# First conditioning of a two-layer mixer kernel: four two-column products at four column tiles in one step

## The chip, the cores and the metric

The kernel runs on one core of one Trainium2 chip. The metric is the device time of the program in microseconds (us). Before the change it is 2925.82 us, the median of three runs (2924.45, 2925.82, 2926.82). A profile of one more execution gives the time of every instruction; the engines in it are PE (matrix products), PEld (loading of the stationary operand of a product), DVE and ACT (elementwise work and copies out of PSUM), POOL (here mostly a queue that issues DMA transfers) and SP (the other such queue).

## The reference, cut to what matters

The program computes two layers of a diffusion backbone over 1024 latent tokens and 256 context tokens, 1024 channels each. The part that changes is the conditioning at the very start. Six vectors of 1024 numbers per layer come out of one product of a conditioning vector with a 1024 x 6144 matrix, and the first two of them (shift and scale) are wanted before the first normalized input exists:

```
def ada_mod(cond, w, b):
    m = (jax.nn.silu(cond) @ w + b)[..., None, :]
    return jnp.split(m, 6, axis=-1)

sh1, sc1, g1, sh2, sc2, g2 = ada_mod(c, ada_w[i], ada_b[i])
u_lat = modulate(rms_norm(h_lat, norm1_g[i]), sh1, sc1)
csh1, csc1, cg1, csh2, csc2, cg2 = ada_mod(c_ctx, ada_w[i], ada_b[i])
u_ctx = modulate(rms_norm(h_ctx, norm1_g[i]), csh1, csc1)
```

There are two conditioning vectors, `c` and `c_ctx`, so the stationary operand of each product has two columns only. In the same stage of the program stands `hyena_filters`: a small network of two sine layers, a product with `w3`, a decaying window, and then the spectrum of the filter, which the kernel makes as products with cosine and sine matrices.

## The kernel before, in words

One class, `Builder`, writes the whole program. A scheduling layer then decides, from the order in which the code is written, from the buffers and from its own costs, in which order each engine receives its instructions; the order inside an engine's queue is fixed from then on, and an engine waits at the head of its queue.

The first 80 us hold four pieces of work, which `run` interleaves by taking steps of generators:

- `ada_first` (L408 to L436). The matrix for scale (m = 1) and shift (m = 0) lies in DRAM as 16 blocks of 128 x 1024 (512 KB each), `in_ada_k`, for two values of m and eight blocks kb of the contraction. Each block goes into a tile `mat`, which takes the two buffers of tag `wh` and the two of tag `wl` in turn, so that four blocks are in the core at a time. The POOL queue issues the loads (`ldr`, L274). For each block there are two products (L416 to L421) with two columns of `cond`, each over 512 of the 1024 outputs, j = 0 and 1, accumulated over kb into two PSUM tiles `ps`. The operands are 32-bit floats. After the eight blocks of m = 1, ACT copies the two rows out of PSUM (L426), eight small products with the identity turn them into columns (L429), and DVE adds the bias. Then the same for m = 0. A generator step is one block; `run` takes eight steps first and then one between any two steps of the filter.
- `filter_mlp` (L561) and `filter_raw` (L607): the sine layers, then 32 products with `w3`, each multiplied by DVE with a window tile `in_win_l` (L641) on its way out of PSUM. `in_win_l` has eight tiles of 256 KB, which the SP queue loads.
- `norms` (in `run`): ten tiles `in_x_row` of 512 KB on the SP queue, squared and summed on ACT (L2144), and three products that spread the result over partitions (`ps` from `t` and `tk`, copied out at L2157).
- `filter_spectrum` (L679): per step, a block of a cosine or sine matrix, `in_ff_l` (256 KB, 16-bit), is loaded by SP into a tile `cs` and cast by ACT to a tile `mat` (L335). These `mat` tiles use the same four buffers as the blocks of `in_ada_k`, and `cs` has two buffers. The operands `s` are made by DVE (L708) and split by ACT (L287) and DVE (L289). Per step come fourteen products, accumulated over b = 0 to 3.

PSUM has six buffers `ps` and two buffers `pq`. Behind this stage stand the second half of the filter spectrum together with the normalized input (L550 to L553), then the input projection from about 202 us on.

Of the kernel before, what the change touches and what calls it, by code (L numbers as in the profile page):

```python
# [10 lines left out]
F32 = mybir.dt.float32  # L11
# [10 lines left out]
KB = D // P  # L22
# [179 lines left out]
class Builder:  # L202
# [205 lines left out]
    def ada_first(self):  # L408

        nc, a = self.nc, self.a  # L410
        cond = self.C(16)
        self.ld(cond, a["cond"])
        nc.scalar.activation(cond, cond, AF.Silu)
        yield
        for m in (1, 0):
            ps = [self.PP(), self.PP()]  # L416
            for kb in range(KB):
                w = self.mat(1024, F32)
                self.ldr(w, a["ada_k"][m, kb])
                for j in (0, 1):  # L420
                    self.mm(ps[j][0:2, :], cond[:, 2 * kb:2 * kb + 2], w[:, j * 512:(j + 1) * 512], kb == 0, kb == KB - 1)  # L421
                yield
            col = self.PS()
            for j in (0, 1):
                row = self.G()
                nc.scalar.copy(row[0:2, :], ps[j][0:2, :])  # L426
                for k in range(4):
                    nb = 4 * j + k
                    self.mm(col[:, 2 * nb:2 * nb + 2], row[0:2, k * P:(k + 1) * P], self.ident[0:2, 0:2], True, True)  # L429
            sl = slice(m * 8, m * 8 + 8)  # L430
            for c in (0, 1):
                t = self.ada[(0, c)]
                nc.vector.tensor_tensor(t[:, sl], col[:, 0:16].rearrange("p (n c) -> p c n", c=2)[:, c],
                                        self.adab[:, sl], ADD)
                if m == 1:
                    nc.vector.scalar_tensor_tensor(t[:, sl], t[:, sl], 1.0, self.gs[:, 0:8], op0=ADD, op1=MUL)  # L436
# [1680 lines left out]
    def run(self):  # L2117
        nc, a = self.nc, self.a
# [10 lines left out]
        def drain(g):  # L2129
            for _ in g:  # L2130
                pass
# [59 lines left out]
        next(fr)  # L2191
        next(ng)
        drain(mlp)
        for _ in range(8):
            next(ada1)
        with self.tc.issue_after(self.clamp), self.tc.issue_after(self.sin):
            next(fr)
# [309 lines left out]
```

## Time and profile before

| | us |
|---|---|
| median of three runs | 2925.82 |
| the profiled execution | 2922.39 |
| its span, first to last instruction | 2920.6 |
| DVE busy | 2094.0 |
| ACT busy | 1647.9 |
| POOL busy | 641.4 |
| mean DMA rate over the span | 211 GB/s |
| mean granted clock of the matrix engine | 0.98 |

The page gives busy time per engine, and then groups of instructions by line, by operation and by tile name, buffer numbers left out. A name at the start of a row is the program's: `mat` is a block of weights, `c` a small constant tile (here `cond`), `s`, `t`, `tk` are working tiles. A 32-bit product is done in two passes, so that one product of the program is two MATMUL rows and two LDWEIGHTS rows of the trace. The granted clock is the share of full speed that the chip gave the matrix engine in a stretch.

### The profile page before, as it was taken

How to read it: one execution, taken by the hardware profiler on the slowest of the kernel's cores; microseconds unless marked ns; L12 is line 12 of the kernel's file. 1: busy time of each engine (PE TensorE's matmuls, PEld its weight loads, DVE VectorE, ACT ScalarE, POOL GpSimd, SP SyncE). 2: the span in 40 equal slices, each digit the busy share in tenths (PEclk: the TensorE clock that was granted, in tenths of full speed). 3: DMA queues.
4: the chain of work that ended last, by engine and by line, in shares of the span. 5: the costliest groups of instructions: out<-in, count | busy, mean ns of one | idle time of the engine just before them, and what ended most of it. 6: DMA issues, size and time to landing. Idle time of an engine off the chain costs nothing. (4 is left out here: it accounts for less than half of the span.)

```text
span 2920.6 us, 46051 instructions
## 1 busy us (share of the span) xinstructions
PE 2777.4 (95%) x16163; PEld 1710.9 (59%) x16163; DVE 2094.0 (72%) x3833; ACT 1647.9 (56%) x2899; POOL 641.4 (22%) x1057
## 2 busy tenths in 40 slices
PE   7889999999989999999999999999999999999998
PEld 3766557878879644444555844677665444444554
DVE  5678867585367798877886777777676778775765
ACT  4675325453675666654555555677664477654553
POOL 1012013354220111123120012454443022112000
PEclk9999999999999999999999999999999999999999
DMA  7574435358685555565995798777775666425753
GB/s 263 182 272 161 156 123 158 110 160 287 257 348 192 207 209 195 201 218 218 332 332 174 267 343 296 171 188 180 184 198 187 238 226 232 152 94 183 237 193 115
DMA packets 325156, 615.98 MB, mean 211 GB/s; under 512 B 90934, under 2 KB 130552, under 8 KB 324922
## 3 DMA queue, kind: packets, MB, share of 16 engines
q1 hardware_dynamic: 252378, 384.38, 40.4%
q0 software_dynamic: 70240, 224.45, 21.5%
q10 hardware_dynamic: 2304, 4.20, 0.4%
q8 instruction: 127, 2.08, 0.3%
q14 instruction: 107, 0.88, 0.1%
HBM read 455.33 MB, written 135.53 MB: 202 GB/s over the span
## 5 line engine op out<-in xcount | busy, mean ns | idle before, releaser
L1444 PE MATMUL ps<-s,s 128*128 128x512 f16 x2592 | 583.2, 382 | 15.8 <-ACT tk L1449 7.2
L1444 PEld LDWEIGHTS <-s 128*128 128x128 f16 x2640 | 258.9, 98 | 334.6 <-issue 30.3
L283 PE MATMUL ps<-s,wh 128*128 128x256 f32 (+3 forms) x1752 | 395.7, 329 | 13.1 <-ACT wh L287 7.3
L1213 ACT ACTIVATE s<-s,c 128x512 f16<-128x512 f32 (+1 forms) x324 | 233.3, 753 | 137.9 <-DMA s<-d 75.8
L1661 PE MATMUL ps<-s 128*128 128x512 f16 (+2 forms) x1308 | 305.0, 379 | 2.0 <-DVE s L1214 2.0
L1214 DVE SCALAR_TENSOR_TENSOR s<-s,c,s 128x512 f16<-128x512 f32 (+1 forms) x324 | 247.4, 794 | 78.3 <-ACT s L1213 77.7
L283 PE MATMUL pq<-s,wh 128*128 128x512 f16 (+1 forms) x1000 | 282.0, 356 | 12.2 <-DMA wh<-d 4.7
L283 PEld LDWEIGHTS <-wh 128*128 128x128 f16 x1664 | 160.3, 99 | 172.7 <-issue 24.7
L283 PE MATMUL ps<-s,wl 128*128 128x256 f32 (+3 forms) x876 | 260.2, 330 | 1.0 <-DVE wl L289 0.9
L274 POOL DMA_DIRECT2D d<-s x201 | 109.0, 543 | 660.5 <-DVE s L1505 193.1
L1661 PEld LDWEIGHTS <-s 128*128 128x128 f16 x1536 | 148.7, 98 | 179.5 <-issue 7.1
L283 PE MATMUL ps<-s,s 128*128 128x65 f16 (+5 forms) x2666 | 220.5, 235 | 20.2 <-DMA s<-s 8.2
L335 ACT CAST mat<-cs 128x1024 fp32r<-128x1024 f16 (+2 forms) x120 | 111.6, 935 | 139.0 <-PE ps L283 56.7
L283 PEld LDWEIGHTS ps<-s,wh 128*128 128x128 f32 x1088 | 178.0, 193 | 20.0 <-ACT wh L287 8.3
L283 PE MATMUL ps<-s,mat 128*128 128x512 f32 x696 | 182.8, 410 | 4.0 <-ACT s L287 3.0
L1444 PE MATMUL ps<-s,wh 128*128 128x512 f16 x616 | 185.0, 379 | 1.5 <-DVE g L1458 1.5
L283 PE MATMUL pq<-s,wl 128*128 128x512 f16 (+1 forms) x500 | 174.9, 355 | 1.6 <-DMA wl<-d 1.1
L283 PEld LDWEIGHTS <-s 128*128 128x128 f16 x2400 | 114.8, 98 | 79.5 <-DMA s<-s 9.1
L283 PEld LDWEIGHTS ps<-s,mat 128*128 128x128 f32 x696 | 135.4, 197 | 38.5 <-ACT s L287 4.4
L1246 ACT ACTIVATE t<-s 128x1024 bf16<-128x1024 f32 (+1 forms) x164 | 141.7, 866 | 14.4 <-DVE c L465 12.1
L1213 ACT ACTIVATE s<-t,c 128x512 f16<-128x512 f32 x172 | 115.1, 712 | 26.1 <-DVE c L1312 15.0
L283 PEld LDWEIGHTS ps<-s,s 128*128 128x128 f32 (+1 forms) x746 | 112.2, 190 | 27.6 <-DVE st L2039 4.2
(431 smaller groups left out, 5449.2 us busy)
## 6 DMA issues: line engine op xcount, KB each, us to landing
s<-d SPq DMA_DIRECT2D x294, 256.0 KB, 4.3
d<-s POOLq DMA_DIRECT2D x157, 256.0 KB, 3.2
s<-in_down SPq DMA_DIRECT2D x154, 256.0 KB, 5.4
s<-in_ada_w POOLq DMA_DIRECT2D x48, 512.0 KB, 5.0
g<-in_bias POOLq DMA_DIRECT2D x128, 192.0 KB, 3.3
s<-in_gate SPq DMA_DIRECT2D x46, 512.0 KB, 3.8
s<-in_up SPq DMA_DIRECT2D x46, 512.0 KB, 3.8
d<-g POOLq DMA_DIRECT2D x87, 256.0 KB, 3.0
```

The lines of the kernel that those rows point to most:

```text
L274: self.last_ldr = self.nc.gpsimd.dma_start(out, in_).ins
L283: self.nc.tensor.matmul(o, l, r, start=st, stop=sp)
L335: self.nc.scalar.copy(m, st)
L1213: nc.scalar.activation(hi, src, AF.Copy, scale=scale)
L1214: nc.vector.scalar_tensor_tensor(lo, src, scale, hi, op0=MUL, op1=SUB)
L1246: self.nc.scalar.activation(junk[:, :t.shape[1]], t, AF.Abs, scale=2.0 ** -15, accum_out=st[:, k:k + 1])
L1444: nc.tensor.matmul(ps, x[:, sl], y, start=first and j == 0 and x is wh and y is xh, stop=j == 3 and x is wl, skip_group_check=True)
L1661: m = nc.tensor.matmul(acc[j][:, c0:c1], x[:, sl], y[:, xs], start=first and k == 0, stop=last and k == 2, skip_group_check=True)
```

## The change

`ada_first` now takes both matrices and both halves in one step: for each kb it loads two blocks and issues four products, which write to four different places of one PSUM tile, partitions 0, 32, 64 and 96. The place of the output selects the columns of the array, so the four products of a step use four different strips of 32 columns. The rows are copied out only when all eight steps are done, first for m = 1 and then for m = 0. `run` takes four steps first, instead of eight, so the number of blocks ahead of the filter is the same.

```
-        for m in (1, 0):
-            ps = [self.PP(), self.PP()]
-            for kb in range(KB):
-                w = self.mat(1024, F32)
-                self.ldr(w, a["ada_k"][m, kb])
+        ps = self.PP()
+        for kb in range(KB):
+            ws = [self.mat(1024, F32) for _ in range(2)]
+            for m in (0, 1):
+                self.ldr(ws[m], a["ada_k"][m, kb])
+            for m in (0, 1):
                 for j in (0, 1):
-                    self.mm(ps[j][0:2, :], cond[:, 2 * kb:2 * kb + 2], w[:, j * 512:(j + 1) * 512], kb == 0, kb == KB - 1)
-                yield
+                    q = 32 * (2 * m + j)
+                    nc.tensor.matmul(ps[q:q + 2, :], cond[:, 2 * kb:2 * kb + 2], ws[m][:, j * 512:(j + 1) * 512],
+                                     start=kb == 0, stop=kb == KB - 1, skip_group_check=True)
+            yield
+        for m in (1, 0):
             col = self.PS()
             for j in (0, 1):
+                q = 32 * (2 * m + j)
                 row = self.G()
-                nc.scalar.copy(row[0:2, :], ps[j][0:2, :])
+                nc.scalar.copy(row[0:2, :], ps[q:q + 2, :])
...
-        for _ in range(8):
+        for _ in range(4):
             next(ada1)
```

Lines of the changed kernel behind this place have numbers five higher (L2157 becomes L2162, L426 becomes L431).

The scheduling layer moves other instructions too. On PE, at the end of these products, before: `ps_275` is the accumulator of m = 0, `mat_391` to `mat_409` are its last three blocks, `ps_366` and `ps_375` spread the norms, `ps_381` and `ps_401` are filter products, and `pq_464` is the first product of the spectrum.

```order
L283 MATMUL ps_366<-tk_361,c_91 128x512
L283 MATMUL ps_375<-tk_370,c_91 128x512
L283 MATMUL ps_275<-mat_391,c_115 2x512
L283 MATMUL ps_276<-mat_391,c_115 2x512
L283 MATMUL ps_381<-s_72_226,s_52_172 128x512
L283 MATMUL ps_381<-s_73_227,s_52_172 128x512
L283 MATMUL ps_275<-mat_405,c_115 2x512
L283 MATMUL ps_276<-mat_405,c_115 2x512
L283 MATMUL ps_401<-s_75_232,s_53_173 128x512
L283 MATMUL ps_401<-s_76_233,s_53_173 128x512
L283 MATMUL ps_275<-mat_409,c_115 2x512
L283 MATMUL ps_276<-mat_409,c_115 2x512
```

And the same place on PE after: `ps_190` is the one accumulator, `ps_346` and `ps_363` receive the columns, then come the three products for the norms and the last four filter products; the spectrum begins behind the last of these rows.

```order
L423 MATMUL ps_190<-mat_329,c_115 2x512 x2
L283 MATMUL ps_346<-c_86,g_347 128x2 x4
L283 MATMUL ps_346<-c_86,g_353 128x2 x4
L283 MATMUL ps_363<-c_86,g_364 128x2 x4
L283 MATMUL ps_363<-c_86,g_370 128x2 x4
L283 MATMUL ps_381<-t_378,c_91 128x256
L283 MATMUL ps_390<-tk_385,c_91 128x512
L283 MATMUL ps_399<-tk_394,c_91 128x512
L283 MATMUL ps_417<-s_71_225,s_53_173 128x512
L283 MATMUL ps_417<-s_72_226,s_53_173 128x512
L283 MATMUL ps_421<-s_74_231,s_53_173 128x512
L283 MATMUL ps_421<-s_75_232,s_53_173 128x512
```

So work that stood among the products of the conditioning now stands behind them: all four groups of columns, the norms and the last filter products.

On the SP queue, at the last two window tiles, before:

```order
L268 DMA s_109_340<-in_win_l 128x512
L268 DMA cs_497<-in_ff_l 128x1024
L268 DMA s_122_379<-in_win_l 128x512
L268 DMA s_128_395<-in_win_l 128x512
L268 DMA cs_521<-in_ff_l 128x1024
L268 DMA cs_549<-in_ff_l 128x1024
```

And at that place of the SP queue after, with the same loads under other numbers:

```order
L268 DMA s_107_336<-in_win_l 128x512
L268 DMA cs_494<-in_ff_l 128x1024
L268 DMA cs_518<-in_ff_l 128x1024
L268 DMA cs_546<-in_ff_l 128x1024
L268 DMA cs_623<-in_ff_l 128x1024
L268 DMA s_125_403<-in_win_l 128x512
L268 DMA s_130_415<-in_win_l 128x512
```

The last two window tiles moved from behind one `in_ff_l` load to behind four. Each of these loads needs a free `cs` buffer, that is, an earlier cast on ACT.

On ACT, between the casts of the first and the fourth matrix block of the spectrum (`mat_456`, `mat_520`), after:

```order
L335 CAST mat_456<-cs_454 128x1024
L335 CAST mat_472<-cs_470 128x1024
L431 COPY g_347<-ps_190 2x512
L431 COPY g_353<-ps_190 2x512
L431 COPY g_364<-ps_190 2x512
L431 COPY g_370<-ps_190 2x512
L335 CAST mat_496<-cs_494 128x1024
L335 CAST mat_520<-cs_518 128x1024
L2162 COPY s_118_383<-ps_381 128x256
L2162 COPY s_121_392<-ps_390 128x512
L2162 COPY s_124_401<-ps_399 128x512
```

Before, two of the four row copies stood earlier, ahead of the norms, and the other two behind the third cast. Now all four stand ahead of the third and the fourth cast, which the SP loads above wait for.

More of the change, by code (lines that the diff above doesn't have):

```diff
@@ L414, in ada_first @@
         yield
-        for m in (1, 0):
-            ps = [self.PP(), self.PP()]
-            for kb in range(KB):
-                w = self.mat(1024, F32)
-                self.ldr(w, a["ada_k"][m, kb])
-                for j in (0, 1):
-                    self.mm(ps[j][0:2, :], cond[:, 2 * kb:2 * kb + 2], w[:, j * 512:(j + 1) * 512], kb == 0, kb == KB - 1)
-                yield
+        ps = self.PP()
[4 more added lines that the diff above has]
+            for m in (0, 1):
+                for j in (0, 1):
+                    q = 32 * (2 * m + j)
+                    nc.tensor.matmul(ps[q:q + 2, :], cond[:, 2 * kb:2 * kb + 2], ws[m][:, j * 512:(j + 1) * 512],
+                                     start=kb == 0, stop=kb == KB - 1, skip_group_check=True)
+            yield
+        for m in (1, 0):
             col = self.PS()
             for j in (0, 1):
+                q = 32 * (2 * m + j)
                 row = self.G()
-                nc.scalar.copy(row[0:2, :], ps[j][0:2, :])
+                nc.scalar.copy(row[0:2, :], ps[q:q + 2, :])
                 for k in range(4):
```

## The prediction

> **What bounds the kernel now.** I read the page first, for the span and the busiest engine.
>
> ```profile
> span 2920.6 us, 46051 instructions
> PE 2777.4 (95%) x16163; PEld 1710.9 (59%) x16163; DVE 2094.0 (72%) x3833; ACT 1647.9 (56%) x2899; POOL 641.4 (22%) x1057
> ```
>
> PE is busy for 95% of the span, so PE time taken out of a stretch in which PE has no gap can reach the end. Then the windows: the first stage in tens of us (the columns after the window are its length and busy time of PE, PEld, DVE, ACT, POOL, then granted clock, DMA share, GB/s), and the stretches behind it.
>
> ```profile
> 20.00:30.00 10.00, 8.89 (x24) 2.61 (x23) 8.18 (x14) 5.92 (x12) 2.69 (x5) 1.00 1.05 409
> 30.00:40.00 10.00, 9.37 (x31) 2.93 (x30) 2.48 (x4) 9.98 (x19) 2.12 (x4) 1.00 1.02 400
> 40.00:50.00 10.00, 10.00 (x34) 4.03 (x34) 8.00 (x20) 3.77 (x12) 1.59 (x3) 1.00 0.45 153
> 50.00:60.00 10.00, 10.00 (x25) 2.59 (x24) 3.10 (x6) 5.45 (x9) 0.53 (x1) 1.00 0.53 181
> 80.00:90.00 10.00, 8.04 (x25) 5.92 (x25) 5.47 (x9) 6.21 (x11) 0.00 (x0) 0.66 0.78 264
> ...
> 81.00:140.00 59.00, 51.40 (x205) 41.41 (x206) 41.13 (x70) 39.83 (x61) 0.00 (x0) 0.88 0.59 195
> 140.00:203.00 63.00, 52.75 (x217) 39.95 (x217) 47.65 (x76) 51.96 (x78) 1.28 (x2) 0.93 0.69 237
> 1000.00:2920.00 1920.00, 1856.55 (x10944) 1010.65 (x10942) 1415.02 (x2576) 1129.91 (x2052) 427.98 (x765) 0.99 0.65 214
> ```
>
> From 40 us on PE is the full one while DMA is half idle; until 40 us DMA is full (share above 1, 400 GB/s) and PE nearly so. Two limits, then: PE, and, where PE gets faster, the loads. From 1000 us on PE is busy 1857 of 1920 us, so a shift made early should be kept.
>
> What PE does in the first stage comes from the groups by form, up to 90 us, and from the order of time on PE:
>
> ```profile
> L283 PE MATMUL ps<-mat,c 128*2 128x512 f32 x64 | 29.4, 597 | 0.0
> L283 PEld LDWEIGHTS ps<-mat,c 128*2 128x2 f32 x64 | 4.6, 84 | 19.0 <-issue 18.3 <-DMA mat<-in_ada_k 0.5
> ...
> 18.85 7.37 PE L283 MATMUL ps<-mat,c 128*2 128x512 f32 x16
> 27.31 0.50 PE L283 MATMUL ps<-s,s 128*128 128x512 f32 x1 [1.09 <-ACT s L287]
> 38.80 1.91 PE L283 MATMUL ps<-c,g 2*128 2x2 f32 x16 [0.30 <-ACT g L426]
> 52.01 0.59 PE L283 MATMUL ps<-t,c 128*128 128x256 f32 x2
> 54.34 1.98 PE L283 MATMUL ps<-tk,c 128*128 128x512 f32 x4
> 61.63 1.45 PE L283 MATMUL ps<-mat,c 128*2 128x512 f32 x3
> 63.01 2.37 PE L283 MATMUL pq<-s,mat 128*128 128x512 f32 x9
> 80.52 0.39 PE L283 MATMUL pq<-s,s 1*128 1x512 f32 x1
> 82.87 0.79 PE L283 MATMUL pq<-s,s 128*128 128x512 f32 x1 [1.96 <-ACT s L287]
> ```
>
> The 32 products are 64 passes, with next to no wait for data (0.5 us), from 18.85 to 63.08. I call 63.1 us the **end of conditioning**. The first part of the spectrum runs from there to 80.9, without a gap; behind it PE waits for ACT. The question is where 80.9 goes.
>
> **The change part by part.**
>
> *The passes.* They follow each other at about 0.43 us (a group of 16 takes 7.37 with its first and last edge), so 64 x 0.43 = 27.5 us of PE. No row of this trace shows two products in the array at once. The lower bound is 27.5 / 4 = 6.9 us, if four products truly run together. One behind the other they stay at 27.5. Above that lies a loss, if each change of strip emptied the array: the edge of a group, 7.37 - 16 x 0.43 = 0.5 us, 32 times, makes 43 us; I leave it out of the cases, since two-column operands already alternate with the stream 64 times without an edge. I take 13.8 us, the middle: the two passes of a product go to the same strip and stand next to each other in the queue, so if the queue keeps its order, only the second pass of one product can run beside the first of the next.
>
> The Trainium skill ("TensorE: Matmul & The Clock Gate", Part 3, "What overlaps and what doesn't") says that matrix products start and end strictly in program order, and its table gives 2.38 times for three column tiles; "TensorEngine Tiling (Array Packing)", Overview, gives up to four as the theoretical gain. By the order rule the sum stays as below; by four times it would be that of the third rival. No row here shows either.
>
> *The loads* set how much of the 13.8 us is used. The POOL queue's issues, and the queue of SP:
>
> ```profile
> L274 POOL DMA_DIRECT2D mat<-in_ada_k x16: 530/530/570, 2.0 to 51.8; - x16
>   PE ps L283: 38.1, 11
> DMA to landing us min/median/max: 3.4/5.8/8.2
> ...
> 31.83 0.53 POOL L274 DMA_DIRECT2D mat<-in_ada_k  x1 [4.78 <-PE ps L283]
> ...
> 33.95 0.69 DVE L641 TENSOR_TENSOR s<-ps,s 128x512 f32<-128x512 f32 x1 [5.21 <-DMA s<-in_win_l]
> ...
> 22.33 7.65 SPq L268 DMA_DIRECT2D s<-in_win_l  x6
> 55.52 0.33 SPq L268 DMA_DIRECT2D cs<-in_ff_l  x1
> 55.89 0.91 SPq L268 DMA_DIRECT2D s<-in_win_l  x2
> ...
> DMA to landing us min/median/max: 2.9/10.1/11.5
> ```
>
> POOL waits 38.1 us, in 11 places, for PE to free a buffer: today PE is behind, and after the change it will be the loads. A block lands 3.4 us after its issue when DMA is quiet, about 8 when it is full. I follow the four rounds of four blocks:
> - Round 1, loaded at 2 us, is used from 18.85 (the sine layers stand ahead of it) to 22.6 instead of 26.2. Round 2 is issued at 20 to 22.6 and lands by about 30, with DMA full.
> - At 27.3 come the filter products, 14 of them in the new order, at some 0.24 us (nine take 2.37 in the row of 63.01, with the edge), to 30.7. Then round 2 is used, to 34.3. Round 3 is issued from 32 on, into the full DMA: 8 us, so it lands at 40.
> - Round 3 is used from 40 to 45.4, with four filter products between (before, PE's next row would have waited for window tiles anyway). Round 4 follows buffer by buffer, issued at 41.4, 43.2, 44.6, 45.5; 3.5 us each gives 45, 46.8, 48.2, 49.1, and 1.3 us of PE behind each.
> - The end of conditioning comes at 51 instead of 63.1: **-12.1 us**. With 27.5 us of passes the same steps give 55, with 6.9 us 48.4.
>
> *What now stands behind the end of conditioning.* Before, 17.8 us led from there to 80.9. After, PE has more to do there: eight more column products (half of the 1.91 row and its other half), the norms (0.59 + 1.98) and four filter products (about 1 us), some 5 us. ACT is as late: four row copies and two casts ahead of the norm copies and of the first operand.
>
> ```profile
> 63.12 0.58 ACT L426 COPY g<-ps 2x512 f32<-2x512 f32 x1 [0.28 <-PE ps L283]
> 58.17 1.05 ACT L335 CAST mat<-cs 128x1024 fp32r<-128x1024 f16 x1 [0.20 <-PE ps L283]
> ```
>
> At 0.5 us in a row for a copy and 1.0 for a cast that is 2.3 + 2.0 us, then three norm copies and two small casts, so the first operand is there 7.6 us behind the end of conditioning. SP's last two window tiles wait for the fourth `in_ff_l`, which waits for the cast that ends at +4.6; they are issued at +5.3 and land at +8.3 (2.9 us). Behind them on DVE stand the splits of operands two and three, in time for PE at +12.4 and +15.7: this wait is hidden, by about 1.5 us, and costs what it exceeds that. From +7.7 the 56 products of this part and the ten short ones behind take 13.4 + 2.4 us at 0.24: the end is at +23.5 instead of +17.8, **+5.7 us**.
>
> *The rest* moves along. Fewer accumulators (one PSUM tile instead of four in all) free buffers that nothing waits for after the first two filter rows. Between 63 and 203 us PE waits six times for ACT or DVE, each time for work of the same stretch:
>
> ```profile
> PE ps L283 <- ACT s L287: 5.4, 2, 2.7
> PE pq L283 <- DVE st L1295: 4.9, 1, 4.9
> ```
>
> None hangs on something at a fixed time. But the scheduling layer swaps a few rows on each engine as far as the first FFN, and the longest of these waits is 4.9 us, so I give each case 4 us to either side.
>
> **Sum**: -12.1 + 5.7 = -6.4 us: 74.5 instead of 80.9, and the profiled execution 2922.4 - 6.4 = 2916.0. The median of the runs shown lies 3.4 us above that execution, so the forecast for it is 2925.8 - 6.4 = **2919.4 us**. About 0.2% (5.9 us) is what a measurement of this kernel can tell from no change; the forecast lies on that line.
>
> **The rivals.**
> - *The strips do not run side by side.* Nothing in the trace speaks for concurrency, the diff alone does. End of conditioning 55, then +5.7: -8.1 + 5.7 = -2.4, 2923.4 us.
> - *All four run together*: 48.4, so -14.7 + 5.7 = -9.0, 2916.8 us. Against it stands the order of the passes.
> - *The gain is taken back by 203 us*, because ACT (52 of the last 63 us) and DVE (48) are the limit there, not PE: 2925.8. For it speaks that PE waits 18 us in that stretch; against it that both were idle for long before 63 us and move along.
> - *Slower: the clock falls.* In 80 to 90 us the granted clock was 0.66 after PE had stood for 1.96 us. A PE that waits for loads from 22.6 to 27 and again between the rounds may run at half speed up to 51. It has about 23 us of work between 18.85 and there (13.8 of passes, 28 filter products, edges); doubled, that ends at 65 instead of 63.1, and with +5.7 the kernel is 7.6 us slower, 2933.4. It decides at a mean clock of about 0.6 in 20 to 51: 23 / 0.6 = 38 us end at 57, and 5.7 more is today's time.
>
> The Trainium skill (same page, Part 1) says that one idle window of some 3.4 us halves the clock and one busy window restores it; the trace agrees with the fall (0.66 after 1.96 us of waiting and smaller gaps). By that rule the wait from 22.6 to 27.3 would halve the clock once, for about 3.4 us, which costs 1.7 us and is hidden by the landing at 40.
>
> **How the numbers follow.** Chances: forecast 0.42, not side by side 0.23, all four 0.18, taken back 0.09, clock 0.08. With 4 us to either side, the forecast is beyond 0.2% in a little over half of its cases, all four in most, not side by side in one of six: faster 0.45, same 0.44, slower 0.11. The range goes from the third rival less 3 us, 2913.5, to the first plus 4.5, 2928; it leaves out the clock and half of the tails. The likeliest case alone gives 2915.4 to 2923.4.
>
> **What would show it.** The 64 passes: their start times, pairs at the same time (sum about 14 us), or fours, or 0.43 us in a row. The last pass at 51, 55 or 48. POOL's waits on PE shrinking and PE's on `in_ada_k` growing from 0.5 us to several. The last short product of the first part at 74.5. The granted clock in 20 to 51. If the first part ends 6 us earlier and the span does not, the loss is behind it, and the first window in which the two traces stop running in parallel shows where. The forecast is wrong if window tiles or `in_ff_l` land later than +8.3, since DVE then holds PE.

## The result, and the profile after

| | before | after |
|---|---|---|
| median of 15 runs each, us | 2925.82 (2915.98 to 2930.05) | 2912.80 (2909.34 to 2922.55) |
| ratio after to before | | 0.9966, 95% interval 0.9955 to 0.9976 |
| the profiled execution, us | 2922.39 | 2919.95 |

The changed kernel is faster by 0.34%, more than the 0.2% that can be told from no change. The ratio puts it at 2915.9 us, 3.5 us under the forecast; the median of its own runs lies 0.7 us under the range. The direction was right. The reason was not, as the rest of this document shows.

From the page of after, span and busiest engines:

```profile
span 2918.2 us, 46050 instructions
PE 2766.6 (95%) x16163; PEld 1714.2 (59%) x16163; DVE 2094.0 (72%) x3833; ACT 1647.7 (56%) x2899; POOL 642.6 (22%) x1057
```

PE has lost 10.8 us of busy time, and the span is 2.4 us shorter. The groups by form of after, up to 90 us, and PE in order of time, show what became of the 64 passes:

```profile
L423 PE MATMUL ps<-mat,c 128*2 128x512 f32 x64 | 13.4, 721 | 5.0 <-DMA mat<-in_ada_k 5.0
...
27.42 0.79 PE L283 MATMUL ps<-s,s 128*128 128x512 f32 x1 [5.86 <-ACT s L287]
32.38 1.90 PE L423 MATMUL ps<-mat,c 128*2 128x512 f32 x16
38.25 1.03 PE L423 MATMUL ps<-mat,c 128*2 128x512 f32 x4 [0.50 <-DMA mat<-in_ada_k]
48.43 1.03 PE L423 MATMUL ps<-mat,c 128*2 128x512 f32 x4 [1.55 <-DMA mat<-in_ada_k]
52.37 3.08 PE L423 MATMUL ps<-mat,c 128*2 128x512 f32 x8 [2.91 <-DMA mat<-in_ada_k]
56.21 6.96 PE L283 MATMUL ps<-c,g 2*128 2x2 f32 x32 [0.77 <-ACT g L431]
69.44 0.39 PE L283 MATMUL ps<-s,c 128*2 128x512 f32 x1 [0.51 <-ACT s L287]
84.57 0.38 PE L283 MATMUL pq<-s,s 1*128 1x512 f32 x1
```

Sixteen passes take 1.90 us where they took 7.37: all four strips run together. PE now waits 5.0 us for the blocks (before 0.5), so the loads do become a limit. A group of sixteen holds four blocks; a block that PE has to wait for comes alone, with four passes for two strips, and takes 1.03 us. But the end of conditioning is at 55.45, not 51, and the first part of the spectrum ends at 84.95. **That is 4 us later than before, not 6.4 earlier.** The windows of the same stretch (length, PE, PEld, DVE, ACT, POOL, granted clock, DMA share, GB/s):

```profile
20.00:30.00 10.00, 4.14 (x20) 2.06 (x11) 8.28 (x14) 5.82 (x12) 2.69 (x5) 0.69 1.04 415
30.00:40.00 10.00, 8.43 (x40) 3.50 (x38) 4.92 (x9) 9.89 (x18) 2.51 (x5) 0.97 1.05 403
40.00:50.00 10.00, 6.53 (x24) 1.27 (x24) 5.90 (x11) 4.58 (x12) 1.71 (x4) 0.83 0.60 214
50.00:60.00 10.00, 6.87 (x26) 4.01 (x27) 0.21 (x3) 4.75 (x7) 0.00 (x0) 0.56 0.28 89
60.00:70.00 10.00, 9.49 (x28) 6.58 (x29) 3.01 (x18) 3.19 (x7) 0.38 (x1) 0.59 0.34 100
70.00:80.00 10.00, 10.00 (x45) 7.54 (x44) 8.70 (x16) 4.25 (x6) 0.00 (x0) 1.00 0.36 105
```

The clock was 1.00 from 20 to 60 us before. Now it is 0.69 to 0.97 while PE waits for the sine layers and the blocks, and 0.56 to 0.59 from 50 to 70, just where all the moved work stands: 32 passes of columns take 6.96 us, where 16 took 1.91 at full clock. POOL and SP, by their tile and in order of time:

```profile
L274 POOL DMA_DIRECT2D mat<-in_ada_k x16: 530/536/570, 2.0 to 46.9; - x16
  PE ps L423: 31.7, 4
DMA to landing us min/median/max: 3.6/6.2/9.9
...
48.00 12.12 SPq L268 DMA_DIRECT2D cs<-in_ff_l  x4
60.17 0.90 SPq L268 DMA_DIRECT2D s<-in_win_l  x2
```

POOL waits less for PE (31.7 us, 38.1 before), and a block lands up to 9.9 us after its issue. The two window tiles are issued at 60.17, 4.7 us behind the end of conditioning.

So this execution is 4 us behind at 85 us and 2.4 us ahead at the end. The gain arises behind the part that the change rewrites.

### The profile page after: what moved, and what is told of

It is laid out like the page before. It is cut to its first block, busy times and chain, and to the rows that moved or that the text cites. A ratio compares the mean times of both kernels' runs of the same rounds, so it can differ in the third digit from the quotient of the medians.

```text
span 2918.2 us, 46050 instructions
## 1 busy us (share of the span) xinstructions
PE 2766.6 (95%) x16163; PEld 1714.2 (59%) x16163; DVE 2094.0 (72%) x3833; ACT 1647.7 (56%) x2899; POOL 642.6 (22%) x1057
## 3 DMA queue, kind: packets, MB, share of 16 engines
q0 software_dynamic: 70240, 224.45, 21.6%
q8 instruction: 127, 2.08, 0.3%
## 5 line engine op out<-in xcount | busy, mean ns | idle before, releaser
L283 PEld LDWEIGHTS <-s 128*128 128x128 f16 x2400 | 114.5, 98 | 82.9 <-DMA s<-s 11.5
L283 PEld LDWEIGHTS <-wl 128*128 128x128 f16 x832 | 82.3, 99 | 77.4 <-issue 4.5
```

What stands on the lines that cost most here:

```text
L283: self.nc.tensor.matmul(o, l, r, start=st, stop=sp)
```

## The experiments

**Theory A:** the gain does not come from the strips. Rewriting the first stage made the scheduling layer put instructions into another order far behind it, and that order waits less. **Theory B:** the strips save the time in the front, and what one profile shows there is chance. **Theory C** came in later: there is no place at all, only steps of the clock that fall one way or another.

The scheduling layer gave a way to take the two apart. Taking seven blocks instead of eight ahead of the filter, in the kernel before, changes little in the first stage, but it gives the changed kernel's order from some 80 us on: the last 25,190 of 25,320 rows of PE and 2,429 of 2,473 of ACT are the same as after. Taking eight steps instead of four in the changed kernel gives before's order behind the strips (23,733 rows of PE, 2,429 of ACT). I call the two orders **old** and **new**.

*e1: no strips, new order.* In the kernel before:

```
-        for _ in range(8):
+        for _ in range(7):
             next(ada1)
```

> The old conditioning, one strip, with seven of its steps first instead of eight. It uses no strips, but the order behind the first 130 or so products is that of the change (25190 of 25320 PE rows at the end are the same rows). Theory A, the rest of the order made the gain: the first stage ends near 81 us as before, what stands behind it takes the time that it takes in the changed kernel, and the whole is as fast as the change or up to 4 us faster, about 2909 to 2913 us against 2926 (ratio 0.994 to 0.9955). Theory B, the strips made the gain: no difference from before, ratio 0.999 to 1.001.

Measured: 2915.94 us beside 2924.80, ratio 0.9972 (0.9959 to 0.9986). The same gain as the whole change, without any strip.

*e2: strips, old order.* In the changed kernel:

```
-        for _ in range(4):
+        for _ in range(8):
             next(ada1)
```

> The new conditioning, four strips, with eight of its steps first. Behind the first stage the order is that of the kernel before (2429 of 2473 ACT rows and 23733 of 25304 PE rows at the end are the same rows). Theory A: the strips alone bring nothing or cost what the profile of the change shows, first part of the spectrum ended 4 us later, so about 2926 to 2930 us, ratio 1.000 to 1.0015. Theory B: as fast as the change, about 2913 us, ratio 0.9955 to 0.997.

Measured: 2923.48 us, 0.9995 (0.9979 to 1.001). No gain that can be told, with the four strips in place.

*e3: the changed kernel again*, no edit.

> The changed kernel once more, for a second profile of its first stage. If the 55.5 us at which its conditioning ended, the clock of 0.56 behind it and the 85 us at which the first part of the spectrum ended are fixed properties, they are seen again within 1 us (Theory A). If they were one bad execution (Theory B), the conditioning ends near 48 us, as worked out for four products together, and the first part of the spectrum near 72 to 75 us. Ratio about 0.9966 either way.

Measured: 2915.66 us, 0.9971 (0.9953 to 0.9989). The front of this profile differs from that of after: end of conditioning 51.94, first part of the spectrum done at 79.19. Neither theory came true: it is not within 1 us of after, and not at 48 and 72 to 75 us. One profile alone does not tell the front to better than some 6 us.

*e4: two strips.* The loop over m of the kernel before, its two halves j in two strips of one accumulator:

```
-            ps = [self.PP(), self.PP()]
+            ps = self.PP()
...
-                    self.mm(ps[j][0:2, :], cond[:, 2 * kb:2 * kb + 2], w[:, j * 512:(j + 1) * 512], kb == 0, kb == KB - 1)
+                    nc.tensor.matmul(ps[32 * j:32 * j + 2, :], cond[:, 2 * kb:2 * kb + 2], w[:, j * 512:(j + 1) * 512],
+                                     start=kb == 0, stop=kb == KB - 1, skip_group_check=True)
```

> The old loop over m, with j = 0 and 1 at two strips of one accumulator: the order stays close to that of before, also behind the first stage. If strips run together, the passes of a block take 2 x 0.43 us instead of 4 x 0.43 us, half of 27.5 us in all. Theory A: loads and the work behind take it back, ratio 0.998 to 1.001. Theory B: PE time saved is time saved, about 13 us, ratio 0.9955.

Measured: 2918.45 us, 0.998 (0.9965 to 0.9996). The first part of the spectrum ends at 77.97, 2.9 us earlier than before; at the places below it has the old order.

**Where the new order is faster.** PE has the same 16,163 recorded passes in every kernel (called products where they are counted from the start), so the time of the n-th marks nearly the same place of the program in each trace. Between profiles of the two orders two stretches differ in time and a third in PE's waits. The clearest is at 870 us, where one product, the spread of a norm (`pq` from `t`), stands at another place in PE's queue. PE before, then e1:

```profile
870.47 1.02 PE L283 MATMUL pq<-t,c 128*128 128x512 f32 x2
876.41 0.79 PE L283 MATMUL ps<-s,wh 128*128 128x256 f32 x2 [4.92 <-ACT wh L287]
877.68 0.58 PE L283 MATMUL ps<-s,wl 128*128 128x256 f32 x1 [0.47 <-DVE wl L289]
```

```profile
861.97 1.02 PE L283 MATMUL pq<-t,c 128*128 128x512 f32 x2
868.25 0.51 PE L283 MATMUL ps<-s,wh 128*128 128x256 f32 x2 [3.07 <-ACT wh L287]
869.51 0.39 PE L283 MATMUL ps<-s,wl 128*128 128x256 f32 x1 [0.75 <-DVE wl L289]
```

And ACT of before at that place:

```profile
871.53 0.59 ACT L524 COPY t<-pq 128x512 f32<-128x512 f32 x1 [0.49 <-PE pq L283]
874.20 1.22 ACT L1340 CAST s<-s 128x512 f16<-128x512 f32 x2 [2.08 <-DVE s L1353]
875.32 2.93 ACT L287 CAST wh<-s 128x1024 fp32r<-128x1024 f32 x3
```

In the old order PE does all its ready products first and the spread last. Then it stands for 4.92 us: ACT copies the result, waits 2.08 us for DVE, which works with the copy, casts twice, and only then comes to the weights `wh` that PE wants. In the new order the spread stands 18 rows earlier, the same chain starts earlier against PE's work, and the wait is 3.07. The wait is 4.92 in all four profiles of the old order and 3.07 in all five of the new. The two products behind it take 0.79 us before and 0.51 in e1, but that is the granted clock of the moment and does not go with the wait: e5 has 0.54 behind 4.92, e11 0.80 behind 3.07. The whole stretch, 4,100 to 4,600 products from the start (844 to 918 us before), is 1 to 3 us shorter. Since the kernel before had one profile only, the next runs give a second one, two other orders, and this one product alone.

*e5: the kernel before, again.*

> The kernel before, a second time, for a second profile. Theory A (the gain lies in the order of the instructions behind the first stage, at places that can be named): ratio 1.000 within 0.0015. At 870 us PE again waits 4.9 us for ACT (wh) in one piece, and 4,100 to 4,600 products from the start take 74.5 to 75 us. From the end of the first part of the spectrum to the input projection 119.8 us as before, with some 10 us lost to a lower granted clock. Theory B (no place; what differs is only where the steps of the clock fall in one execution): the last length moves by several us from one profile to the other, to 117 as well as to 122, and with it the lost clock.

Measured: 0.9997 (0.9983 to 1.001). The wait at 870 is 4.92 us again. From 220 to 630 products it takes 116.6 us, with 12.7 lost to the clock, where the first profile of the same kernel has 115.5 and 8.4.

*e6: five blocks ahead of the filter* (`range(5)` in the kernel before).

> The kernel before with five blocks of the conditioning ahead of the filter. By the program's order the one product of the norm at 870 us stands where it did before, while from there to the end PE has the changed kernel's order. Theory A: the wait of 4.9 us at 870 is there, so 2.8 us of the gain of e1 (8.9 us) is missing; if the rest comes with the order behind 870 us the ratio is 0.998, if it comes from the stretch between 80 and 200 us it is between 0.998 and 1.000. Theory B: any value between 0.997 and 1.001.

Measured: 2919.64 us beside 2925.74, 0.9983 (0.9965 to 1.0): some 60% of e1's gain, with the long stretch at 870 us as in the old order (75.6 us) and the new order behind it. The interval reaches 1, and in its profile 1.7 us are gained in the front already (first part done at 79.19), so it does not say where the gain lies.

*e7: twelve blocks* (`range(12)`).

> The kernel before with twelve blocks ahead of the filter; the order is that of before from about 250 us to the end. Theory A: 1.000 within 0.0015, the wait of 4.9 us at 870 is there. If everything came from the first 200 us, the ratio would be off 1 by as much as the input projection starts earlier or later than 200.7 us in its profile.

Measured: 2924.88 us, 0.9994 (0.998 to 1.0008). Between 88 and 204 us it gains 3 us on before, and it has lost as much ahead of that.

*e8: the one product.* In the kernel before, the third block of the products with `up` in the FFN's second step is issued behind the spread, so that the spread goes 18 rows forward on PE. Nothing else changes there on PE; some rows of DVE and ACT follow.

```
-        self.mm(ps[:, :w], self.ones, t[:, :w], True, True)
+        self.rms_mm = nc.tensor.matmul(ps[:, :w], self.ones, t[:, :w], start=True, stop=True).ins
...
-            for w, part in ((wh, 0), (wh, 1), (wl, 0)):
+            with self.follow(behind if i == 2 else None):
+                for w, part in ((wh, 0), (wh, 1), (wl, 0)):
...
-                ua = self.lin(uh, ul, 0, range(KB), u, (2,))[2]
+                ua = self.lin(uh, ul, 0, range(KB), u, (2,), behind=self.rms_mm if fb == 1 else None)[2]
```

> The kernel before with one product on PE (the spread of a norm over the partitions, at 870 us) 18 rows earlier, where the changed kernel has it; a few rows of DVE and ACT follow. Nothing else is changed. Theory A: PE's wait for ACT (wh) there goes from 4.9 to 3.1 us, 4,100 to 4,600 products from the start take 71.9 instead of 74.5 us, and the kernel is 2.6 us faster: ratio 0.999. Theory B: ratio 1.000, since what is saved there is given back.

Measured: 2923.62 us, 0.9987 (0.9974 to 1.0). PE and then ACT in its trace:

```profile
863.82 1.13 PE L523 MATMUL pq<-t,c 128*128 128x512 f32 x2 [0.24 <-ACT t L521]
871.12 0.50 PE L283 MATMUL ps<-s,wh 128*128 128x256 f32 x2 [4.04 <-ACT wh L287]
...
865.08 0.94 ACT L1525 ACTIVATE t<-ps 128x256 f32<-128x256 f32 x3
865.89 0.61 ACT L525 COPY t<-pq 128x512 f32<-128x512 f32 x1
```

The wait falls by 0.9 us, not by 1.85. On ACT the copy stands behind three activations, and starts 2.1 us after the product, where e1 has it after 1.06. So the wait does hang on the place of this product, and PE's row alone is worth about half of what the new order takes off it. In time this step cannot be told: the stretch takes 73.5 us, and e10 below, with the old order and the full wait, takes 73.7; the ratio does not tell 0.9987 from 1.

The last runs repeat the corners and add a candidate.

*e9: two strips, four blocks ahead of the filter* (e4 with `range(4)`): PE's order is the new one from some 310 us on.

> Before's loop over m with two strips per block (as e4), four blocks ahead of the filter. Here the conditioning is that of e4, and the order from some 280 us to the end is that of the changed kernel on PE, the one product at 870 us included. Theory A (the gain belongs to the order): what e1 gained behind 100 us (about 8 us) and what e4 gained ahead of it (2.5 us) add up, 2914 to 2916 us where before shows 2925, ratio 0.9965; 4,100 to 4,600 products take 72 us. Theory B (it is chance of the clock, or hangs on the strips): 0.998 as e4 again.

Measured: 2908.87 us (6 runs) beside 2926.89, 0.994 (0.9924 to 0.9956): **faster than both kernels**. Its front gains more than I expected. PE in order of time, SP's queue, and the windows:

```profile
32.37 3.60 PE L421 MATMUL ps<-mat,c 128*2 128x512 f32 x16
53.45 1.03 PE L421 MATMUL ps<-mat,c 128*2 128x512 f32 x4 [0.18 <-DMA mat<-in_ada_k]
56.60 1.55 PE L283 MATMUL ps<-s,mat 128*128 128x512 f32 x6
72.44 0.38 PE L283 MATMUL pq<-s,s 1*128 1x512 f32 x1
...
21.98 10.97 SPq L268 DMA_DIRECT2D s<-in_win_l  x8
52.67 5.70 SPq L268 DMA_DIRECT2D cs<-in_ff_l  x4
...
50.00:60.00 10.00, 9.14 (x46) 4.34 (x44) 8.08 (x14) 8.45 (x13) 0.00 (x0) 1.00 0.49 156
60.00:70.00 10.00, 10.00 (x46) 7.83 (x46) 6.85 (x20) 3.15 (x3) 0.38 (x1) 1.00 0.39 123
```

The conditioning ends at 54.5, hardly earlier than after. But all eight window tiles are issued ahead of the `in_ff_l` loads, the spectrum starts 2 us behind the last pass, the clock is 1.00 from 50 to 70, and the first part ends at 72.8, 8.1 us earlier than before.

*e10: e2 again.*

> The same kernel as e2 (four strips, the order of before behind the first stage), for a second profile and a second ratio. Theory A: 0.9995 within 0.0015 again; in the profile 4,100 to 4,600 products take 74.9 us, and from 220 to 630 products (88 to 203 us) over 115 us with more than 10 us lost to the clock. Theory B: the ratio moves to 0.997 or 0.998, and the lost clock of that stretch to 5 to 9 us.

Measured: 2921.47 us, 0.998 (0.9966 to 0.9995); 114.8 us with 9.8 lost, and 73.7 us at the place of 870. It gains a little more than e2 and lies at the edge of what theory A allowed, with both stretches slightly under it.

*e11: e1 again.*

> The same kernel as e1 (no strips, the order of the changed kernel behind the first stage), for a second profile. Theory A: 0.997 within 0.0015; 71.9 us for 4,100 to 4,600 products; under 114 us from 220 to 630 products, with under 10 us lost to the clock. Theory B: nearer to 1, and 115 us or more there.

Measured: 2915.98 us, 0.9961 (0.9947 to 0.9976); 113.0 us with 5.3 lost, 72.5 us. Its front shows a fall of the clock without any wait of PE:

```profile
38.77 1.94 PE L283 MATMUL ps<-c,g 2*128 2x2 f32 x16
...
30.00:40.00 10.00, 10.00 (x33) 3.04 (x33) 5.25 (x8) 9.98 (x19) 2.12 (x4) 1.00 1.05 413
40.00:50.00 10.00, 10.00 (x30) 3.66 (x30) 6.30 (x17) 3.56 (x12) 1.05 (x2) 0.83 0.35 131
```

PE is busy for 10.00 of 10 us in both windows, and by the records of the granted clock it was 0.50 from 41.4 to 44.8, 0.7 us behind sixteen passes of columns (2x2 operands). e1 has the same fall at 40.8; before, with these passes at 38.80, has none.

*e12: the changed kernel, third profile.*

> The changed kernel, a third profile. Theory A: 0.997 within 0.0015, 71.9 us and under 115 us in the two stretches. For the front: the end of conditioning at 52 to 55.5 us and the first part of the spectrum at 79 to 85 us, that is, between 2 us earlier and 4 us later than before, by how far the clock falls in 50 to 70 us; if the fall is not by chance but belongs to the kernel, the mean granted clock between 50 and 70 us is below 0.9 again.

Measured: 2915.96 us, 0.9966 (0.995 to 0.9982); 72.1 us and 114.3 us. The end of conditioning is at 53.7, the first part ends at 82.9, and the clock is 0.74 and 0.75 in the two windows from 50 to 70. In three profiles of the changed kernel the first part ends at 79.2, 82.9 and 85.0, with 80.9 before: the low clock belongs to this front, its depth varies.

**Together.** Mean span and mean granted clock are known for every run. "Lost" is span times one minus clock: an upper bound of what the clock cost, since it also falls while PE waits. The kernel before is taken over the three sets, e5 included. With 95% intervals:

| | old order | new order |
|---|---|---|
| no strips: span, us | 2923.9 ± 0.9 (103 runs) | 2913.7 ± 1.8 (e1, e11; 18 runs) |
| lost | 59.8 ± 0.9 | 53.3 ± 2.0 |
| four strips: span, us | 2920.2 ± 2.2 (e2, e10; 24 runs) | 2914.3 ± 1.9 (after, e3, e12; 37 runs) |
| lost | 63.5 ± 2.0 | 62.7 ± 1.9 |

The order is worth 10.2 ± 2.0 us without the strips and 5.9 ± 2.9 us with them. The strips are worth 3.7 ± 2.4 us under the old order, and nothing that can be told under the new one (+0.6 ± 2.6). What the clock did not take shows them better: span less lost falls by 7.4 us (2864.1 to 2856.7) and by 8.8 (2860.4 to 2851.6) with the strips, and the lost share rises by 3.7 and 9.4. **By this bound the strips free up to 7 or 9 us, and the clock takes half of it back, or all**; both are upper figures, since the clock that falls while PE waits for loads is in them. By the same bound the order's 10.2 us are up to 6.5 of lost clock and 3.7 of the rest, and its 5.9 us with the strips 0.8 and 5.1: without the strips, most of what the order gains may be clock and not waits.

Where the order gains, from the records of one profile each (us; stretches by products from PE's start, with the times of before):

| | 0 to 220 (7 to 88 us) | 220 to 630 (to 204) | of it lost | 4,100 to 4,600 (844 to 918) | PE idle 4,600 to 6,800 (to 1,348) |
|---|---|---|---|---|---|
| old: before | 81.4 | 115.5 | 8.4 | 74.5 | 11.3 |
| old: e5 | 80.8 | 116.6 | 12.7 | 75.0 | 11.6 |
| old: e2, strips | 80.9 | 116.8 | 12.7 | 74.9 | 13.0 |
| old: e10, strips | 82.1 | 114.8 | 9.8 | 73.7 | 11.9 |
| new: e1 | 82.0 | 112.6 | 5.1 | 71.9 | 10.8 |
| new: e11 | 81.7 | 113.0 | 5.3 | 72.5 | 10.6 |
| new: after, strips | 85.3 | 114.5 | 9.5 | 72.1 | 10.0 |
| new: e3, strips | 79.5 | 111.7 | 6.5 | 71.9 | 9.9 |
| new: e12, strips | 82.5 | 114.3 | 9.6 | 72.1 | 10.1 |
| e9, two strips | 72.9 | 116.6 | 12.5 | 72.9 | 10.7 |

In the last four columns every value of the new order is below every one of the old, but for the lost clock, where they meet (9.6 and 8.4). The means differ by 2.7 us from 220 to 630, by 2.4 at the place of 870 and by 1.7 of idle behind it. The idle is not gained in time: from 4,600 to 6,800 products the old order takes 427.9 us in the mean and the new one 427.4. So these places hold some 5.5 us. Outside the four corners the first of these columns does not follow the order so cleanly: e7 takes 112.4 us there, with rows in an order of its own. The waits view has the last two by name, for the stretches 844 to 918.5 and 918.5 to 1347.7 of before, and the same of after:

```profile
PE ps L283 <- ACT wh L287: 7.3, 2, 4.9
...
PE ps L1444 <- ACT g L1449: 5.5, 4, 2.9
```

```profile
PE ps L283 <- ACT wh L287: 5.4, 2, 3.1
...
PE ps L1449 <- ACT g L1454: 4.2, 3, 2.9
```

The first stretch is another matter, as its windows show for before, e5, after and e11 (one row each):

```profile
88.10:203.60 115.50, 99.52 (x412) 77.53 (x411) 84.48 (x137) 87.98 (x130) 1.28 (x2) 0.93 0.63 213
```

```profile
87.50:204.10 116.60, 102.32 (x412) 79.63 (x412) 85.02 (x139) 87.76 (x129) 1.28 (x2) 0.89 0.65 216
```

```profile
92.30:206.80 114.50, 98.92 (x412) 77.58 (x411) 84.37 (x137) 88.04 (x130) 1.28 (x2) 0.92 0.63 215
```

```profile
88.40:201.40 113.00, 96.30 (x411) 75.12 (x411) 84.16 (x138) 88.22 (x130) 1.28 (x2) 0.95 0.64 218
```

The work is the same and PE waits no less (16.0, 14.3, 15.6 and 16.7 us); the same 411 or 412 products take 96 to 102 us of PE, as the clock allows. So theory C holds for a part: what the new order gains here comes by way of the clock.

## Why the prediction came out as it did

*The bound and the loads: right.* PE was the limit of the front, and with faster products the loads are: PE's waits for blocks went from 0.5 to 5.0 us, POOL's waits for PE from 38.1 to 31.7. The window tiles, the wait that the prediction called hidden by 1.5 us, were issued at +4.7 instead of +5.3, and PE did not wait for DVE's splits behind them; its longest wait there is 0.51 us, for ACT. (Two small sums of the prediction do not come out: its steps to the end of conditioning add up to 50.4, not 51, and the third rival less 3 us is 2913.8, not 2913.5. Nothing hangs on either.)

*The passes: wrong.* "I take 13.8 us, the middle", because the two passes of a product would keep the queue in pairs. The total of 13.4 us agrees only by accident. Sixteen passes in 1.90 us are four at a time, the rival with 0.18, and make 7.6 us for all 64; but a block that PE has to wait for fills only two strips (1.03 us for four passes), and the low clock adds to that. By the Trainium skill ("TensorE: Matmul & The Clock Gate", Part 3), matrix products start and end in program order and three column tiles give 2.38 times; here four gave 7.37 / 1.90 = 3.9 times. The starts do not speak against that order: in the group at 32.38 four passes start at 32.382, 32.389, 32.396 and 32.402, and the next four together 0.43 us behind them. What failed is my step from the order to pairs, for four products that start in turn within 0.02 us run side by side all the same.

*The end of conditioning at 51: about right, for another reason.* Measured are 55.5, 51.9 and 53.7, and 49.9 and 50.9 with the old order. With all four together I had 48.4. PE was through round 1 at 21.6 and then stood 5.86 us for the first filter operand, to 27.4 as the sum has it, so the faster passes bought nothing there. What was mis-sized is the last round: in after its four blocks were issued at 39.6, 44.7, 46.3 and 46.9, the last of them 1.4 us later than in the sum, and landed 3.6 to 6.7 us after issue (3.6 to 4.6 in e3, 3.6 to 5.9 in e12), where they were priced at 3.5.

*Behind the end of conditioning, +5.7 us: the term that failed in the front.* From the end of conditioning to the end of the first part it takes 29.5, 27.3 and 29.3 us, not 23.5. I had counted the moved work, columns, norms and filter products, at full clock. The mean granted clock over these stretches was 0.78, 0.87 and 0.81, and 29.5, 27.3 and 29.3 us at that clock are 23.0, 23.7 and 23.7 at full clock (an estimate, since PE also waited for 1.3 to 1.6 us of them): the work was priced about right, and the clock is the term that the sum left out. By the records of the granted clock it fell to 0.50 at 51 to 55 us in all three and stayed there for 17.1, 6.8 and 10.2 us; the 32 passes of columns took 6.96, 4.70 and 6.60 us. By the Trainium skill ("TensorE: Matmul & The Clock Gate", Part 1) an idle window of some 3.4 us halves the clock and a busy one restores it; the fall in 20 to 30 us agrees (in after PE stood from 21.6 to 27.4, and the clock was 0.50 from 23.8 to 30.6). The 17.1 us at half agree only if the passes of columns do not count as busy, since by the profile PE was busy for 9.49 us of 60 to 70; for it speak the fall behind such passes in e11, and that the half clock ended 5.0, 4.6 and 4.1 us behind the last of them in the three profiles. No run takes these passes away, so this stays open.

The rival of the clock named the mechanism and put it at the wrong place, 20 to 51 us, with the chance of 0.08; it came behind that, from 50 to 70. The row on which that rival rested was misread: by the records the clock of before fell at 81.0 us, when the wait of 1.96 us had just begun (80.91), not after it; so this fall does not bear out the rule of the idle window, as the prediction had it. By the end of the first part the front stood at +4.0, -1.7 and +2.0 us in three profiles, not at -6.4. Over all runs the strips gave 0 to 4 us.

*"The rest moves along", within 4 us: the term that made the result.* I saw that rows were swapped as far as the first FFN, and gave them the size of the longest wait that I saw between 63 and 203 us. The swaps gave 10.2 us without the strips, 5.9 with them, and the largest that can be named stands at 870 us, where a wait for ACT of 4.92 us stands outside the stretch whose waits I had read.

So the forecast of -6.4 was near the measured -10 by the sum of two errors: the strips' gain arrived in part at most (3.7 us on the old order, none that can be told on the new), and an unpriced order brought 5.9 to 10.2. It was a fit of the time, not of the mechanism.

*What stays open.* Why the clock falls less between 88 and 204 us in the new order is not settled; PE waits there no less. The named stretches hold some 5.5 us; what the order gains beyond them (10.2 without the strips) is not located, since the tail of one profile scatters by more than that. By the rows of the traces of before and after, PE's order differs for the last time at 1,093 us and ACT's at 1,806. That e9 beats the changed kernel by the front is read from one profile of it; its order between 88 and 310 us is its own.

## What to carry over

Where a scheduler sorts the program, an edit of the first 60 us can change the order at 870 us, and the changed order can be worth more than the edit: build the pair "old code with the new order" and "new code with the old order" before the edit gets the credit. Take the swapped rows to the longest waits of the whole trace, not only to those near the edit. And when faster products leave an engine waiting for loads, price the work that was pushed behind them at the clock that it will get, or keep that work between the waits, as e9 does.

## What the runs showed of the hardware that I had not expected

- Column strips ran fully side by side for 32-bit products of two passes each: 16 passes took 7.37 us in one strip, 3.60 in two, 1.90 in four. One block by itself, four passes in two strips, took 1.03.
- What the profile counts as busy did not keep the clock up: in e11 PE was busy for 10.00 us of 40 to 50, and the clock was 0.50 from 41.4 to 44.8, behind sixteen passes over 2x2 operands. In after PE was busy for 9.49 us of 60 to 70, with no wait over 0.51 us, and was granted 0.59; it was 1.00 in the next 10 us.
- The lost clock of a whole run is large beside the effects studied: 53 to 64 us in the mean of the four corners. An order without added work or strips moved it by 6.5 us.
